# Written order on ACT and VectorE in one group of an up projection and in the last two products, and one ring of tiles for two kinds of data

## The chip, the cores and the metric

One core of a Trainium2 chip runs the whole program. The metric is the device time of one execution in microseconds (us); the profile below is of one such execution, and its times count from the start of its span.

## The reference

One decoder layer on 1024 tokens of width 1024, in float32: a token mixer, then an MLP with squared ReLU (up to 4096, back to 1024), then a last RMSNorm. The change touches the MLP and the last norm:

```python
x = x + jnp.concatenate([y_pool, y_hgrn], axis=-1) @ w_out[l]
h2 = rms_norm(x, norm_mlp_g[l])
x = x + jnp.square(jax.nn.relu(h2 @ w_up[l])) @ w_down[l]
return rms_norm(x, final_norm_g)
```

## The kernel before, in words

**Arithmetic.** Each float32 operand is split into a high part, a cast on ACT (`split`, L116), and a low part, a subtraction on VectorE (L117). A product is then three matmuls: high by high, high by low, low by high (`mm3`, L122 to L124), so the third one (L124) needs the low part of the weights. Both matrix products of the MLP are done in groups of seven products by Strassen's scheme. Sums and differences of quarters are formed first, and the seven results are added into four quarters.

**Up projection.** The hidden width is cut into 8 groups. A group has seven products, each with 24 matmuls of 128x512 in two PSUM banks. Group 0 takes them in the order 1, 2, 5, 6, 3, 7, 4; the others in 1, 5, 6, 3, 7, 2, 4. Product n needs an operand made of quarters of h2.T (`operand(n)`, tiles `h2op_n`) and one made of w_up (`up_weights(n)`: a sum `wsum` or `wdif`, then the split into `whi`, `wlo`). The h2 operands are made once, around group 0, from four tiles `quad`, each 128 x 4 x 512, that `mlp_input` fills with transposes from PE and `mixed_blocks` turns into the sums. For 5 that happens row block by row block; for 6, 3, 7 and 4 as whole tiles of 2048 columns.

**Results of a product.** `sums_out` takes them out of PSUM: ACT copies a bank (products 1, 5, 6; L869 where the profile names it), VectorE adds a bank to what is there (2, 7, 3), product 4 goes through ReLU. Products 1, 6, 7 and 4 use the banks `ps_ua`, 5 and 3 the banks `ps_uc`, 2 the banks `ps_ub`. A later product adds onto what its banks hold, so it may start only when the result of the earlier one has been taken out: product 6 waits for the copies of 1, 3 for those of 5, 7 for those of 6, and 4 for the adds of 7. Finished quarters (`h11`, `h22`, `h12`, `h21`, and the sums `hs3`, `hs2`, `hs4`) go to DRAM over POOL's queue. In the kernel before they have a pool of their own, `hq`, of eight tiles of 128 x 2 x 512, and the pool `quadp` ends when group 0's operands are made.

**Down projection.** Four groups of seven products with 48 matmuls each, in four banks, in the order 1, 5, 3, 6, 7, 2, 4. Their results are added into x, row block by row block. In the last group the row blocks become final one after another. Then come the square sum of the row (ACT, L925), its mean (VectorE, L699 and L701), the power -1/2 (POOL, L704), the scaling of the left half (VectorE, L940) and of the right half (ACT, L938), and two stores.

**Order of the work.** PE's order is written by hand throughout (`manual_schedule`). ACT's, VectorE's and POOL's order in the two projections is chosen by the scheduler that builds the program. Every engine runs its instructions in that fixed order. An instruction that waits for a semaphore holds up what stands behind it on its engine.

Of the kernel before, what the change touches and what calls it, by code (L numbers as in the profile page):

```python
# [10 lines left out]
F32 = mybir.dt.float32  # L11
# [6 lines left out]
P = 128  # L18
# [42 lines left out]
def kernel(  # L61
# [605 lines left out]

    rawp = tc.alloc_tile_pool(name="rawp", bufs=2, reuse_waits="tile")
    sums = tc.alloc_tile_pool(name="sums", bufs=2, reuse_waits="tile")
    with ExitStack() as pb:  # L670
        quadp = pb.enter_context(tc.tile_pool(name="quadp", bufs=4, reuse_waits="tile"))
        g2 = bcast_row(norm_mlp_g, "g2")


# [63 lines left out]
        def mixed_blocks(i):  # L738


            b11, b12, b21, b22 = (quad[k][:, :, i % 4 * P:(i % 4 + 1) * P] for k in ((0, 0), (0, 1), (1, 0), (1, 1)))
            sub(b11, b12, b11)
            split(*(t[:, :, i % 4 * P:(i % 4 + 1) * P] for t in h2[5]), b11)
            sub(b11, b22, b11)
            sub(b12, b22, b12)
            sub(b21, b21, b11)

        def product_out(step, dh):
# [89 lines left out]
        operand(3, big, quad[1, 1])  # L838
        operand(7, big2, quad[0, 1])
        operand(4, big2, quad[1, 0])  # L840

    with ExitStack() as pc:
        hq = pc.enter_context(tc.tile_pool(name="hq", bufs=8, reuse_waits="tile"))

        def up_group(g, order):
            if g:
# [4 lines left out]
            c = {}  # L851
            store, at = hid_out[g // 2], slice(g % 2 * 2, g % 2 * 2 + 2)

            def quarter(name):
                return hq.tile([P, 2, 512], F32, tag="hq", name=f"{name}_{g}")

            def relu2(t):
                dve.scalar_tensor_tensor(out=t, in0=t, scalar=0.0, in1=t, op0=ALU.max, op1=ALU.mult)
# [56 lines left out]
    with ExitStack() as pd:  # L915
# [5 lines left out]
        xs, sss = [None] * NT, [[] for _ in range(NT)]  # L921

        def squares(i, cs, name):
            ss = small.tile([P, 1], F32, tag="ss3", name=f"ss3_{i}_{name}", bufs=16)
            act.activation(junk[:, :cs.stop - cs.start], xs[i][:, cs], AF.Square, accum_out=ss)  # L925
            sss[i].append(ss)

        def final_scale(i, dh, y):
            cs = slice(dh * 512, (dh + 1) * 512)
            dve.tensor_tensor(out=y[:, cs], in0=xs[i][:, cs], in1=gf[:, cs], op=ALU.mult)  # L930

        def final_rows(i, y):

            r = rstd_of_parts(sss[i], f"n3_{i}")
            for h in range(2):
                cs = slice(h * 512, (h + 1) * 512)
                if h:
                    act.mul(y[:, cs], y[:, cs], r)  # L938
                else:
                    dve.scalar_tensor_tensor(out=y[:, cs], in0=xs[i][:, cs], scalar=r, in1=gf[:, cs], op0=ALU.mult, op1=ALU.mult)  # L940
                (nc.sync, act)[h].dma_start(out[0, i * P:(i + 1) * P, cs], y[:, cs])
# [40 lines left out]
        groups, banks, ys, scales, finals = {}, {}, {}, [], []
        products = [(g, n) for g in range(DOWN_GROUPS) for n in DOWN_ORDER]
        ahead = operands(*products[0])
        for at, (g, n) in enumerate(products):
            last = g == DOWN_GROUPS - 1
            pools, a, b = ahead
            if at + 1 < len(products):
                ahead = operands(*products[at + 1])
            if last and n == DOWN_ORDER[-2]:  # L990
                for i in scales:
                    final_scale(i, 1, ys[i])
# [4 lines left out]
            for e in range(4):  # L997
                ps, tc_ = banks[g, key][e], slice(e * P, (e + 1) * P)
                for k in range(4):
                    mm3(ps, (a[0][:, k, tc_], a[1][:, k, tc_]), (b[0][:, k, :], b[1][:, k, :]), fresh and k == 0, k == 3, not fresh)  # L1000

                for i, dh in {1: [(e, 0)], 5: [(e + 4, 1)], 3: [(e, 1)], 6: [(e, 1)], 7: [(e + 4, 1)], 2: [(e, 0)], 4: [(e + 4, 0)]}[n]:
                    cs = slice(dh * 512, (dh + 1) * 512)
                    add(xs[i][:, cs], ps, xs[i][:, cs])
                    if last and n in (6, 7, 2, 4):
                        squares(i, cs, dh)

                        ys[i] = groups[g][0][i // 4][:, i % 4, :]
                        if n in (6, 7):
                            scales.append(i)  # L1010
                        else:
                            finals.append(i)
                            if len(finals) > 1:
                                final_rows(finals[-2], ys[finals[-2]])
# [58 lines left out]
```

## Time and profile before

| | |
|---|---|
| median of 3 runs | 1109.58 us (1108.75 to 1110.09) |
| the profiled execution's own time | 1108.45 us |
| its span | 1106.7 us |
| PE busy | 1082.3 us, 98% of the span |
| VectorE busy | 790.9 us, 71% |
| ACT busy | 422.6 us, 38% |
| up projection, group 0 | about 476.7 to 525 us |
| rest of up, and down | 525 to 1095.6 us |
| after the last matmul | 1095.6 to 1106.7 us |

The time of a run is the span and what lies around it, here 1.75 us. PE's busy time counts matmuls that overlap one another, so 98% says only that PE seldom stands still. In the rows, L with a number is a line of the kernel before; PE is the matmul engine, DVE is VectorE, ACT is ScalarE, POOL is GpSimd.

### The profile page before, as it was taken

The page shows a single profiled execution, that of the slowest core. Times are in us where ns is not written, and L with a number is a line of the kernel's source. Part 1 is how long each engine was busy: PE and PEld are TensorE (multiplying, and loading weights), DVE is VectorE, ACT ScalarE, POOL GpSimd, SP SyncE. Part 2 cuts the span into 40 slices and gives each one's busy share as a digit, 9 for nine tenths or more (in the row PEclk, how much of TensorE's full clock was granted, in tenths as well). Part 3 has the DMA queues.
Part 4 walks back from the last instruction along what each step waited for, and adds up shares of the span by engine and source line. Part 5 has one row for each costly group of instructions (what it writes and reads, how often), then busy time and mean ns, then how long its engine had stood idle before and what let it go on. Part 6 is the DMA issues. An engine that isn't in the chain of part 4 may idle for free.

```text
span 1106.7 us, 14288 instructions
## 1 busy us (share of the span) xinstructions
PE 1082.3 (98%) x5728; PEld 895.0 (81%) x5728; DVE 790.9 (71%) x1068; ACT 422.6 (38%) x647; POOL 81.9 (7%) x124
## 2 busy tenths in 40 slices
PE   8999999999999999999999999999999999999996
PEld 6868797879787788877888888888888888888884
DVE  4498837784779852698568557855988968677774
ACT  6844333434332522353332233224244333324243
POOL 1001010101010111100011001001100000000001
PEclk9999999999999999999999999999999999999998
DMA  9521011110110162324354344427984354353104
GB/s 310 157 58 38 21 39 38 40 38 20 58 39 20 58 219 96 105 77 132 115 190 171 107 159 176 148 95 264 366 344 166 114 190 152 114 197 145 38 1 152
DMA packets 71362, 137.55 MB, mean 124 GB/s; under 512 B 4864, under 2 KB 44928, under 8 KB 67712
## 3 DMA queue, kind: packets, MB, share of 16 engines
q1 hardware_dynamic: 60656, 100.98, 26.8%
q0 software_dynamic: 9344, 33.56, 7.8%
q10 hardware_dynamic: 1296, 2.10, 0.5%
q8 instruction: 45, 0.74, 0.3%
q14 instruction: 21, 0.17, 0.1%
HBM read 98.87 MB, written 37.75 MB: 123 GB/s over the span
## 4 chain that ended last, share of the span: by engine, by line
PE 78%; DVE 12%; issue 3%; ACT 2%; DMA 2%; POOL 1%; SPq 0%; POOLq 0%; DVEq 0%; ACTq 0%
PE ps_dx L122 5%; PE ps_dx L124 5%; PE ps_dx L123 5%; PE ps_ua L122 5%; PE ps_ua L123 5%; PE ps_ua L124 5%; PE ps_dy L122 3%; PE ps_dy L124 3%; PE ps_dy L123 3%; PE ps_uc L123 2%; PE ps_uc L122 2%; PE ps_uc L124 2%; PE ps_o L122 2%; PE ps_o L123 2%; PE ps_o L124 2%
## 5 line engine op out<-in xcount | busy, mean ns | idle before, releaser
L116 ACT CAST wdop<-raw_wd 128x2048 fp32r<-128x2048 f32 x28 | 53.5, 1912 | 154.4 <-PE ps_dy L124 47.2
L122 PE MATMUL ps_ua<-h2op,whi_wu 128*128 128x512 f32 x256 | 100.1, 391 | 3.2 <-ACT h L869 2.7
L123 PE MATMUL ps_ua<-h2op,whi_wu 128*128 128x512 f32 x256 | 99.7, 389 | 0.0
L124 PE MATMUL ps_ua<-h2op,wlo_wu 128*128 128x512 f32 x256 | 99.7, 389 | 0.0
L123 PE MATMUL ps_dx<-wdop,hop 128*128 128x512 f32 x256 | 99.6, 389 | 0.0
L124 PE MATMUL ps_dx<-wdop,hop 128*128 128x512 f32 x256 | 99.6, 389 | 0.0
L122 PE MATMUL ps_dx<-wdop,hop 128*128 128x512 f32 x256 | 99.6, 389 | 0.0
L117 DVE TENSOR_TENSOR wdop<-raw_wd,wdop 128x2048 fp32r<-128x2048 f32 x28 | 64.1, 2290 | 28.6 <-ACT wdop L116 28.6
L117 DVE TENSOR_TENSOR wlo_wu<-raw_wu,whi_wu 128x1024 fp32r<-128x1024 f32 x24 | 29.2, 1222 | 55.0 <-ACT whi_wu L116 55.0
L117 DVE TENSOR_TENSOR hop<-hraw,hop 128x2048 fp32r<-128x2048 f32 x28 | 63.9, 2283 | 4.5 <-ACT hop L116 4.5
L116 ACT CAST hop<-hraw 128x2048 fp32r<-128x2048 f32 x28 | 53.4, 1909 | 30.7 <-DMA hraw<-hid 22.4
L116 ACT CAST whi_wu<-wsum 128x1024 fp32r<-128x1024 f32 x24 | 25.3, 1054 | 99.3 <-DVE wsum L659 49.0
L122 PEld LDWEIGHTS ps_ua<-h2op,whi_wu 128*128 128x128 f32 x256 | 48.1, 188 | 14.2 <-ACT h L869 3.1
L124 PEld LDWEIGHTS ps_dx<-wdop,hop 128*128 128x128 f32 x256 | 48.1, 188 | 10.0
L124 PEld LDWEIGHTS ps_ua<-h2op,wlo_wu 128*128 128x128 f32 x256 | 48.1, 188 | 10.0
L123 PEld LDWEIGHTS ps_dx<-wdop,hop 128*128 128x128 f32 x256 | 48.1, 188 | 10.0
L122 PE MATMUL ps_v<-whi_v,hT_hi 128*128 128x256 f32 x192 | 54.5, 285 | 1.6 <-ACT whi_v L116 1.5
L122 PEld LDWEIGHTS ps_dx<-wdop,hop 128*128 128x128 f32 x256 | 48.1, 188 | 9.9
L123 PEld LDWEIGHTS ps_ua<-h2op,whi_wu 128*128 128x128 f32 x256 | 48.1, 188 | 9.8
L662 DVE TENSOR_TENSOR x<-ps_dx,x 128x512 f32<-128x512 f32 x64 | 43.9, 686 | 16.4 <-PE ps_dx L124 16.4
L123 PE MATMUL ps_v<-wlo_v,hT_hi 128*128 128x256 f32 x192 | 54.3, 284 | 0.8 <-DVE wlo_v L117 0.8
L124 PE MATMUL ps_v<-whi_v,hT_lo 128*128 128x256 f32 x192 | 54.1, 284 | 0.0
(230 smaller groups left out, 2779.2 us busy)
## 6 DMA issues: line engine op xcount, KB each, us to landing
hraw<-hid SPq DMA_DIRECT2D x28, 1024.0 KB, 5.3
raw_wu<-in_w_up_dram SPq DMA_DIRECT2D x32, 512.0 KB, 3.7
hid<-h POOLq DMA_DIRECT2D x32, 512.0 KB, 3.2
raw_wd<-in_w_down_dram SPq DMA_DIRECT2D x16, 1024.0 KB, 7.2
hid<-hs POOLq DMA_DIRECT2D x24, 512.0 KB, 3.4
xt<-in_x_t_dram SPq DMA_DIRECT2D x8, 512.0 KB, 7.8
xn<-in_x_dram SPq DMA_DIRECT2D x8, 512.0 KB, 6.8
x<-x_mid SPq DMA_DIRECT2D x8, 512.0 KB, 6.5
```

Of the source, the lines that this page charges most:

```text
L116: act.copy(hi, src)
L117: dve.tensor_tensor(out=lo, in0=src, in1=hi.bitcast(F32), op=ALU.subtract)
L122: pe.matmul(ps, lh, rh, start=start, stop=False, skip_group_check=goes_on)
L123: pe.matmul(ps, lh, rl, start=False, stop=False, skip_group_check=goes_on)
L124: pe.matmul(ps, ll, rh, start=False, stop=stop, skip_group_check=goes_on)
L662: dve.tensor_tensor(out=out_, in0=a, in1=b, op=ALU.add)
```

## The change

There are three parts. First, the hidden quarters no longer have a pool: `quadp` lives through the whole up projection, and a quarter is one half of a tile of that ring of four. Pairs share a tile: h11 and h22; h12 and hs3; h21 and hs4; hs2 has one alone. Second, in group 0 ACT and VectorE run in the order in which the code is written. `up_weights(6)` now stands ahead of the last `mlp_input`, operand 6 ahead of the first results, and operands and weights of 3, 7 and 4 are each written one product ahead of their use. Third, the last two down products have written order on VectorE, ACT and POOL; a row's mean starts from a right half that was worked out earlier, and the rows 4 to 7 are put out from a tile `y` of their own.

```diff
+    quadp = tc.alloc_tile_pool(name="quadp", bufs=4, reuse_waits="tile")
...
-        quadp = pb.enter_context(tc.tile_pool(name="quadp", bufs=4, reuse_waits="tile"))
...
             sub(b11, b12, b11)
+            sub(b12, b22, b12)
             split(*(t[:, :, i % 4 * P:(i % 4 + 1) * P] for t in h2[5]), b11)
             sub(b11, b22, b11)
-            sub(b12, b22, b12)
             sub(b21, b21, b11)
...
+        steady = tc.manual_schedule(engines={mybir.EngineType.DVE, mybir.EngineType.Activation})
+        steady.__enter__()
         for n, key in ((1, "a"), (2, "b")):
...
             if n == 1:
+                split_first[6] = up_weights(0, 6, w_first, s_first)
                 mlp_input(7)
                 mixed_blocks(7)
-        operand(6, big, quad[0, 0])
-        split_first[6] = up_weights(0, 6, w_first, s_first)
-        operand(3, big, quad[1, 1])
-        operand(7, big2, quad[0, 1])
-        operand(4, big2, quad[1, 0])
-
-    with ExitStack() as pc:
-        hq = pc.enter_context(tc.tile_pool(name="hq", bufs=8, reuse_waits="tile"))
+
+        later = {6: (big, quad[0, 0]), 3: (big, quad[1, 1]), 7: (big2, quad[0, 1]), 4: (big2, quad[1, 0])}
...
             def quarter(name):
-                return hq.tile([P, 2, 512], F32, tag="hq", name=f"{name}_{g}")
+
+                place = {"h11": 0, "h22": 0, "h12": 1, "hs3": 1, "hs2": 2, "h21": 3, "hs4": 3}[name]
+                if place not in pairs:
+                    pairs[place] = [quadp.tile([P, 2, 2, 512], F32, tag="quad", name=f"hid_{g}_{place}"), 0]
+                t, n = pairs[place]
+                pairs[place][1] += 1
+                return t[:, n]
...
-            for n in order:
+            for at_, n in enumerate(order):
                 key = {1: "a", 6: "a", 7: "a", 4: "a", 5: "c", 3: "c", 2: "b"}[n]
+                if g == 0:
+                    for m in order[3:at_ + 3] or order[3:4]:
+                        if m in later:
+                            operand(m, *later.pop(m))
+                            if m not in ready:
+                                ready[m] = up_weights(g, m, w, s)
                 if g == 0 and n in (1, 2):
...
             up_group(g, ORDER if g else FIRST_ORDER)
+            if g == 0:
+                steady.__exit__(None, None, None)
+    quadp.release()
...
+        def right_half(i, y):
+
+            ss = small.tile([P, 1], F32, tag="part", name=f"ss_{i}", bufs=8)
+            dve.tensor_scalar(ss, squares(i, 1), 1.0 / D, EPS, op0=ALU.mult, op1=ALU.add)
+            sss[i] = ss
+            ys[i] = y
+            dve.tensor_tensor(out=y[:, 512:], in0=xs[i][:, 512:], in1=gf[:, 512:], op=ALU.mult)
+
+        def row_scale(i, ss):
+            ms = small.tile([P, 1], F32, tag="ms", name=f"ms_n3_{i}")
+            dve.tensor_scalar(ms, ss, 1.0 / D, sss[i], op0=ALU.mult, op1=ALU.add)
...
+                rows = [groups[g][0][0], places.pop(0).tile([P, 4, D], F32, tag="big", name="y")]
...
+        with tc.manual_schedule(engines={mybir.EngineType.DVE, mybir.EngineType.Activation, mybir.EngineType.Pool}):
+            pools, a, b = ahead
+            ahead = operands(*products[-1])
+            ready = None
+            for (g, n), (pools, a, b) in zip(products[-2:], ((pools, a, b), ahead)):
+                for i in product(g, n, a, b):
+                    ss = squares(i, 0)
+                    if ready:
+                        final_rows(*ready)
+                    ready = i, row_scale(i, ss)
+            final_rows(*ready)
```

The order that results on ACT, in group 0, from where VectorE forms the last h2 sums (whi_wu_0_n: high part of the weights of product n in group 0; h2op_n: operand n; h11_0, h22_0, h12_0: hidden quarters). Before:

```order
L116 CAST h2op_5_4179<-quad_00_3702 128x4x128
L116 CAST h2op_7_4476<-quad_01_3700 128x2048
L116 CAST h2op_6_4465<-quad_00_3702 128x2048
L116 CAST h2op_3_4473<-quad_11_3703 128x2048
L116 CAST h2op_4_4479<-quad_10_3701 128x2048
L869 COPY h11_0_4486<-ps_ua_0_0_4395 128x512
L869 COPY h11_0_4486<-ps_ua_0_1_4396 128x512
L869 COPY h22_0_4507<-ps_uc_0_0_4493 128x512
L869 COPY h22_0_4507<-ps_uc_0_1_4494 128x512
L116 CAST whi_wu_0_3_4550<-wsum_0_4389 128x1024
L116 CAST whi_wu_0_7_4583<-wdif_0_4581 128x1024
L116 CAST whi_wu_0_4_4623<-raw_wu_0_11_4379 128x1024
```

And of the change, where hid_0_0 is the tile of h11 and h22, and hid_0_1 that of h12:

```order
L116 CAST h2op_6_4472<-quad_00_3702 128x2048
L872 COPY hid_0_0_4475<-ps_ua_0_0_4397 128x512
L872 COPY hid_0_0_4475<-ps_ua_0_1_4398 128x512
L116 CAST h2op_3_4482<-quad_11_3703 128x2048
L116 CAST whi_wu_0_3_4486<-wsum_0_4389 128x1024
L872 COPY hid_0_0_4475<-ps_uc_0_0_4490 128x512
L872 COPY hid_0_0_4475<-ps_uc_0_1_4491 128x512
L116 CAST h2op_7_4518<-quad_01_3700 128x2048
L116 CAST whi_wu_0_7_4523<-wdif_0_4521 128x1024
L872 COPY hid_0_1_4539<-ps_ua_0_0_4397 128x512
L872 COPY hid_0_1_4539<-ps_ua_0_1_4398 128x512
L116 CAST h2op_4_4554<-quad_10_3701 128x2048
```

The four casts of h2 stood in a row, ahead of the copies out of PSUM and of the weights of 3, 7 and 4; now those of 3, 7 and 4 stand each just ahead of the weights of the same product, and copies lie between.

VectorE in group 0, up to its first add of product 7 (the one that frees the bank in which product 4 starts; wlo is the low part of weights, wsum_1, wdif_1 and wlo_wu_1_n belong to group 1). Before:

```order
L858 SCALAR_TENSOR_TENSOR h11_0_4486<-h11_0_4486 128x1024
L117 TENSOR_TENSOR wlo_wu_0_3_4551<-wsum_0_4389,whi_wu_0_3_4550 128x1024
L117 TENSOR_TENSOR wlo_wu_0_7_4584<-wdif_0_4581,whi_wu_0_7_4583 128x1024
L117 TENSOR_TENSOR wlo_wu_0_4_4624<-raw_wu_0_11_4379,whi_wu_0_4_4623 128x1024
L117 TENSOR_TENSOR wlo_wu_1_1_4671<-raw_wu_1_00_4660,whi_wu_1_1_4670 128x1024
L662 TENSOR_TENSOR wsum_1_4703<-raw_wu_1_10_4664,raw_wu_1_11_4666 128x1024
L662 TENSOR_TENSOR h12_0_4534<-ps_uc_0_0_4493,h12_0_4534 128x512
L659 TENSOR_TENSOR wdif_1_4800<-raw_wu_1_00_4660,raw_wu_1_10_4664 128x1024
L662 TENSOR_TENSOR h12_0_4534<-ps_uc_0_1_4494,h12_0_4534 128x512
L858 SCALAR_TENSOR_TENSOR h12_0_4534<-h12_0_4534 128x1024
L117 TENSOR_TENSOR wlo_wu_1_5_4706<-wsum_1_4703,whi_wu_1_5_4705 128x1024
L662 TENSOR_TENSOR h22_0_4507<-ps_ua_0_0_4395,h22_0_4507 128x512
```

And of the change:

```order
L659 TENSOR_TENSOR wsum_0_4389<-raw_wu_0_01_4375,wsum_0_4389 128x1024
L117 TENSOR_TENSOR wlo_wu_0_3_4487<-wsum_0_4389,whi_wu_0_3_4486 128x1024
L117 TENSOR_TENSOR h2op_7_4518<-quad_01_3700,h2op_7_4518 128x2048
L659 TENSOR_TENSOR wdif_0_4521<-raw_wu_0_00_4373,raw_wu_0_10_4377 128x1024
L117 TENSOR_TENSOR wlo_wu_0_7_4524<-wdif_0_4521,whi_wu_0_7_4523 128x1024
L117 TENSOR_TENSOR h2op_4_4554<-quad_10_3701,h2op_4_4554 128x2048
L117 TENSOR_TENSOR wlo_wu_0_4_4558<-raw_wu_0_11_4379,whi_wu_0_4_4557 128x1024
L662 TENSOR_TENSOR hid_0_1_4539<-ps_uc_0_0_4490,hid_0_1_4539 128x512
L662 TENSOR_TENSOR hid_0_1_4539<-ps_uc_0_1_4491,hid_0_1_4539 128x512
L117 TENSOR_TENSOR wlo_wu_1_1_4667<-raw_wu_1_00_4656,whi_wu_1_1_4666 128x1024
L861 SCALAR_TENSOR_TENSOR hid_0_1_4539<-hid_0_1_4539 128x1024
L662 TENSOR_TENSOR hid_0_0_4475<-ps_ua_0_0_4397,hid_0_0_4475 128x512
```

The low parts of 3, 7 and 4 stood side by side, and three instructions for group 1 (wsum_1, wdif_1, wlo_wu_1_5) lay ahead of the last row; now the h2 subtractions of 7 and 4 lie between the low parts, and the three instructions for group 1 come later.

VectorE at the end of the program (x_i: row block i; rstd_n3_i: its scale; ps_dx: the banks of the last product). Before:

```order
L699 TENSOR_SCALAR ms0_n3_7_8337<-ss3_7_1_8124 128x1
L940 SCALAR_TENSOR_TENSOR raw_wd_3_1_7736<-x_6_6461,rstd_n3_6_8331,gf_6441 128x512
L662 TENSOR_TENSOR x_7_6463<-ps_dx_3_3_7811,x_7_6463 128x512
L701 SCALAR_TENSOR_TENSOR ms1_n3_7_8339<-ss3_7_0_8325,ms0_n3_7_8337 128x1
L940 SCALAR_TENSOR_TENSOR raw_wd_3_1_7736<-x_7_6463,rstd_n3_7_8341,gf_6441 128x512
```

And of the change:

```order
L950 TENSOR_SCALAR ms_n3_6_8294<-ss3_6_0_8288,ss_6_8103 128x1
L662 TENSOR_TENSOR x_7_6438<-ps_dx_3_3_7786,x_7_6438 128x512
L957 SCALAR_TENSOR_TENSOR y_7973<-x_6_6436,rstd_n3_6_8296,gf_6416 128x512
L950 TENSOR_SCALAR ms_n3_7_8317<-ss3_7_0_8311,ss_7_8121 128x1
L957 SCALAR_TENSOR_TENSOR y_7973<-x_7_6438,rstd_n3_7_8319,gf_6416 128x512
```

The add of row block 7 stood behind the scaling of row block 6, and stands ahead of it now.

## Rows read from the trace of the kernel before

**Rows 1.** The page's first part: busy time of each engine over the span, its share, and the number of instructions.

```profile
PE 1082.3 (98%) x5728; PEld 895.0 (81%) x5728; DVE 790.9 (71%) x1068; ACT 422.6 (38%) x647; POOL 81.9 (7%) x124
```

**Rows 2.** [...]

```profile
476.70:506.70 30.00, 25.55 (x119) 20.59 (x118) 29.21 (x31) 19.90 (x24) 1.73 (x3) 1.00 0.26 89
506.70:510.10 3.40, 3.40 (x9) 2.66 (x9) 2.38 (x3) 0.27 (x1) 0.00 (x0) 0.51 0.45 120
...
525.00:1095.60 570.60, 570.60 (x2518) 472.31 (x2516) 418.78 (x390) 196.66 (x194) 31.44 (x59) 1.00 0.45 163
1095.60:1106.70 11.10, 0.02 (x1) 0.00 (x0) 2.49 (x6) 2.72 (x6) 1.08 (x2) 0.73 0.38 142
```

**Rows 3.** What PE waited for between 476 and 525 us: total, times, longest.

```profile
PE ps_ua L122 <- ACT h L869: 2.7, 1, 2.7
PE ps_uc L124 <- DVE wlo_wu L117: 1.8, 1, 1.8
PE ps_ua L122 <- DVE h L662: 0.5, 1, 0.5
```

**Rows 4.** PE's instructions in group 0, in order of time: start, duration, what it is, and in brackets the idle time before it and its releaser.

```profile
494.63 0.39 PE L124 MATMUL ps_uc<-h2op,wlo_wu 128*128 128x512 f32 x1
497.69 0.50 PE L122 MATMUL ps_ua<-h2op,whi_wu 128*128 128x512 f32 x1 [2.68 <-ACT h L869]
...
505.73 0.50 PE L124 MATMUL ps_uc<-h2op,wlo_wu 128*128 128x512 f32 x1 [1.78 <-DVE wlo_wu L117]
...
507.20 0.63 PE L123 MATMUL ps_uc<-h2op,whi_wu 128*128 128x512 f32 x1
507.63 0.63 PE L124 MATMUL ps_uc<-h2op,wlo_wu 128*128 128x512 f32 x1
...
512.46 0.39 PE L122 MATMUL ps_ua<-h2op,whi_wu 128*128 128x512 f32 x1
...
517.67 0.39 PE L124 MATMUL ps_ua<-h2op,wlo_wu 128*128 128x512 f32 x1
518.55 0.50 PE L122 MATMUL ps_ua<-h2op,whi_wu 128*128 128x512 f32 x1 [0.49 <-DVE h L662]
```

**Rows 5.** VectorE in group 0, in the same form; x4 or x2 marks neighbours that are merged into one row.

```profile
492.06 8.89 DVE L117 TENSOR_TENSOR h2op<-quad,h2op 128x2048 fp32r<-128x2048 f32 x4
500.87 1.22 DVE L659 TENSOR_TENSOR wsum<-raw_wu,wsum 128x1024 f32<-128x1024 f32 x1
...
503.32 1.23 DVE L858 SCALAR_TENSOR_TENSOR h<-h 128x1024 f32<-128x1024 f32 x1
...
506.73 2.35 DVE L117 TENSOR_TENSOR wlo_wu<-raw_wu,whi_wu 128x1024 fp32r<-128x1024 f32 x2
511.94 1.23 DVE L662 TENSOR_TENSOR wsum<-raw_wu,raw_wu 128x1024 f32<-128x1024 f32 x1 [2.86 <-DMA raw_wu<-in_w_up_dram]
...
513.68 1.22 DVE L659 TENSOR_TENSOR wdif<-raw_wu,raw_wu 128x1024 f32<-128x1024 f32 x1
...
516.68 1.22 DVE L117 TENSOR_TENSOR wlo_wu<-wsum,whi_wu 128x1024 fp32r<-128x1024 f32 x1
517.81 0.68 DVE L662 TENSOR_TENSOR h<-ps_ua,h 128x512 f32<-128x512 f32 x1
```

**Rows 6.** ACT in group 0, in the same form.

```profile
486.89 1.05 ACT L116 CAST whi_wu<-wsum 128x1024 fp32r<-128x1024 f32 x1 [2.10 <-DVE wsum L659]
...
489.83 7.33 ACT L116 CAST h2op<-quad 128x2048 fp32r<-128x2048 f32 x4 [1.37 <-DVE quad L659]
497.06 1.06 ACT L869 COPY h<-ps_ua 128x512 f32<-128x512 f32 x2
...
502.12 1.05 ACT L116 CAST whi_wu<-wsum 128x1024 fp32r<-128x1024 f32 x1 [2.20 <-DVE wsum L659]
```

**Rows 7.** DMA issues: KB of each, and median us from issue to landing.

```profile
raw_wu<-in_w_up_dram SPq DMA_DIRECT2D x32, 512.0 KB, 3.7
hid<-h POOLq DMA_DIRECT2D x32, 512.0 KB, 3.2
```

**Rows 8.** All engines at the end of the program, in order of time; ACTq is the queue of DMAs that ACT issues.

```profile
1094.72 0.68 DVE L662 TENSOR_TENSOR x<-ps_dx,x 128x512 f32<-128x512 f32 x1
...
1095.23 0.39 PE L124 MATMUL ps_dx<-wdop,hop 128*128 128x512 f32 x1
...
1097.00 0.72 ACT L938 ACTIVATE raw_wd<-raw_wd,rstd_n 128x512 f32<-128x512 f32 x1 [0.84 <-POOL rstd_n L704]
1097.00 0.75 DVE L940 SCALAR_TENSOR_TENSOR raw_wd<-x,rstd_n,gf 128x512 f32<-128x512 f32 x1 [0.59 <-POOL rstd_n L704]
1097.67 0.68 DVE L662 TENSOR_TENSOR x<-ps_dx,x 128x512 f32<-128x512 f32 x1
...
1098.39 0.63 ACT L925 ACTIVATE junk<-x 128x512 bf16<-128x512 f32 x1 [0.67 <-DVE x L662]
...
1099.14 0.16 DVE L701 SCALAR_TENSOR_TENSOR ms_n<-ss,ms_n 128x1 f32<-128x1 f32 x1 [0.79 <-ACT junk L925]
1099.38 0.54 POOL L704 TENSOR_TENSOR rstd_n<-ms_n,nhalf 128x1 f32<-128x1 f32 x1 [2.41 <-DVE ms_n L701]
1099.95 0.72 ACT L938 ACTIVATE raw_wd<-raw_wd,rstd_n 128x512 f32<-128x512 f32 x1 [0.85 <-POOL rstd_n L704]
...
1100.71 0.37 ACTq L941 DMA_DIRECT2D out_dram<-raw_wd  x1
```

More of the change, by code (lines that the diff above doesn't have):

```diff
@@ L850, in up_group @@
                 w, banks, s, ready = w_first, dict(first), s_first, split_first
-            c = {}
+            c, pairs = {}, {}
             store, at = hid_out[g // 2], slice(g % 2 * 2, g % 2 * 2 + 2)
             def quarter(name):
-                return hq.tile([P, 2, 512], F32, tag="hq", name=f"{name}_{g}")
+                place = {"h11": 0, "h22": 0, "h12": 1, "hs3": 1, "hs2": 2, "h21": 3, "hs4": 3}[name]
[4 more added lines that the diff above has]
+                return t[:, n]
             def relu2(t):
@@ L920 @@
         places = [big, big, big, big2, big2, big, big2]
[L921 to L941, printed above, removed]
+        xs, sss = [None] * NT, [None] * NT
@@ new lines, in squares @@
+        def squares(i, dh):
+            ss = small.tile([P, 1], F32, tag="ss3", name=f"ss3_{i}_{dh}", bufs=16)
+            act.activation(junk, xs[i][:, dh * 512:(dh + 1) * 512], AF.Square, accum_out=ss)
+            return ss
+        def right_half(i, y):
[4 more added lines that the diff above has]
+            dve.tensor_tensor(out=y[:, 512:], in0=xs[i][:, 512:], in1=gf[:, 512:], op=ALU.mult)
@@ new lines, in row_scale, with final_rows @@
+        def row_scale(i, ss):
+            ms = small.tile([P, 1], F32, tag="ms", name=f"ms_n3_{i}")
+            dve.tensor_scalar(ms, ss, 1.0 / D, sss[i], op0=ALU.mult, op1=ALU.add)
+            r = small.tile([P, 1], F32, tag="rstd", name=f"rstd_n3_{i}")
+            pool.tensor_tensor(out=r, in0=ms, in1=nhalf[:, :1], op=ALU.pow)
+            return r
+        def final_rows(i, r):
+            y = ys[i]
+            dve.scalar_tensor_tensor(out=y[:, :512], in0=xs[i][:, :512], scalar=r, in1=gf[:, :512], op0=ALU.mult, op1=ALU.mult)
+            act.mul(y[:, 512:], y[:, 512:], r)
+            nc.sync.dma_start(out[0, i * P:(i + 1) * P, :512], y[:, :512])
+            act.dma_start(out[0, i * P:(i + 1) * P, 512:], y[:, 512:])
@@ L980, in operands, with product @@
             return pools, a, b
[L982 to L992, printed above, removed]
+        def product(g, n, a, b):
             key = "y" if n in (5, 3) else "z" if n == 2 else "x"
@@ L1000 @@
                     mm3(ps, (a[0][:, k, tc_], a[1][:, k, tc_]), (b[0][:, k, :], b[1][:, k, :]), fresh and k == 0, k == 3, not fresh)
[L1002 to L1014, printed above, removed]
+                i, dh = {1: (e, 0), 5: (e + 4, 1), 3: (e, 1), 6: (e, 1), 7: (e + 4, 1), 2: (e, 0), 4: (e + 4, 0)}[n]
+                cs = slice(dh * 512, (dh + 1) * 512)
+                add(xs[i][:, cs], ps, xs[i][:, cs])
+                yield i
+        groups, banks, ys = {}, {}, {}
+        products = [(g, n) for g in range(DOWN_GROUPS) for n in DOWN_ORDER]
+        ahead = operands(*products[0])
+        for at, (g, n) in enumerate(products[:-2]):
+            last = g == DOWN_GROUPS - 1
+            pools, a, b = ahead
+            ahead = operands(*products[at + 1])
+            if last and n == 6:
+                rows = [groups[g][0][0], places.pop(0).tile([P, 4, D], F32, tag="big", name="y")]
+            for i in product(g, n, a, b):
+                if last and n in (6, 7):
+                    right_half(i, rows[i // 4][:, i % 4, :])
             places += pools
@@ L1017 @@
                 places.append(groups[g][1].pop(0))
-        final_rows(finals[-1], ys[finals[-1]])
+        with tc.manual_schedule(engines={mybir.EngineType.DVE, mybir.EngineType.Activation, mybir.EngineType.Pool}):
+            pools, a, b = ahead
+            ahead = operands(*products[-1])
+            ready = None
+            for (g, n), (pools, a, b) in zip(products[-2:], ((pools, a, b), ahead)):
+                for i in product(g, n, a, b):
+                    ss = squares(i, 0)
[3 more added lines that the diff above has]
+            final_rows(*ready)
 _INS = [
```

## The prediction

> **What bounds the kernel now.** I began with the totals. PE is busy for 1082.3 of 1106.7 us, VectorE for 790.9 and ACT for 422.6 [rows 1]. An average hides stages with different limits, so the next view was the busy time by stretch. From 525 to 1095.6 us PE is busy for the whole 570.60 us [rows 2]. No edit there that leaves the matmuls alone can bring the end forward; it can only bring a stop. That leaves two places: group 0 of the up projection, and the end.
>
> In group 0 the waits name three stops of PE: 2.7 us for a copy of h11 by ACT, 1.8 us for the low part of a weight, 0.5 us for an add of VectorE [rows 3]. The timeline shows where: ahead of products 6 (497.69) and 3 (505.73), and ahead of 4 (518.55). In between is a stretch without any wait in which matmuls start 0.43 us apart (507.20, 507.63), where product 7 has 23 steps in 5.21 us, 0.227 each [rows 4]. [...] From the last matmul of product 5 (494.63) to the first of product 4 there are 73 steps, 16.6 us at 0.227; they took 23.9. So 7.4 us is lost: the three waits, about 1.6 us of slow clock (8 steps at 0.2 us extra), and the restarts.
>
> Why PE waits is seen on the other two. VectorE has no gap worth naming from 492 to 509; four h2 subtractions in a row take 8.89 us [rows 5]. ACT casts the same four in 7.33 us, and the copies that product 6 wants stand behind them, at 497.06 [rows 6]. So it is a matter of order on two full engines, and the account to draw up is VectorE's.
>
> At the end, the last matmul starts at 1095.23 and is done 0.39 us later. VectorE, though, scales row block 6 first (1097.00) and adds the last bank at 1097.67. From there the square (1098.39), the mean (1099.14), the power (1099.38), the scaling (1099.95) and the last store (1100.71) follow in a chain [rows 8].
>
> **Group 0 after the change.** Unit prices, all from [rows 5, 6]: VectorE 0.68 us for 512 columns, 1.22 for 1024, 2.22 for 2048 in a row (8.89/4); ACT 0.53 for a copy (1.06/2), 1.05 for a cast of 1024, 1.83 for one of 2048 (7.33/4). A hand-off costs 0.03 to 0.05: VectorE ends the sum of 500.87 at 502.09, ACT starts at 502.12. VectorE's work from 482 us to the add that frees product 4's bank is the same as before, but for three instructions of group 1 that the written order puts behind it (wsum_1, wdif_1, wlo_wu_1_5). They are the rows at 511.94, 513.68 and 516.68: 3 x 1.14 from start to start, 3.4 us. With them goes the 2.86 us that the first of them waited for a load. Without new gaps that add, which ended at 518.49, would end at 518.49 - 2.86 - 3.4 = 512.2.
>
> Now the gaps that the written order makes. Wherever VectorE's next instruction needs a cast that itself needs VectorE's last one, it stands still for the cast and two hand-offs. Going down the new order:
> first, wlo of 6 needs whi of 6, which needs the sum just made: 1.05 + 0.1, less 0.6 for a subtraction that runs meanwhile, 0.55;
> second, h2op_6 needs a cast of 2048 that starts when the last sum is there: 1.9, less 0.6 of other work, 1.3;
> third, the h11 adds need ACT's copy, which begins once h2op_6 is done (the ring gives the tile only then): 0.53 + 0.1, about 0.7;
> fourth and sixth, wlo of 3 and of 7: each needs the cast of a sum made just before, 1.05 + 0.1 = 1.15, twice 2.3;
> fifth and seventh, h2op_7 and h2op_4: ACT does two copies (1.06) and the cast (1.83) after whi, 2.8 with the hand-offs, while VectorE has only a wlo of 1.22 to do, 1.6, twice 3.2.
> These are 8.05 us. The instruction ahead of each gap takes its full duration and not its step to the next start (1.22 against 1.14, 0.68 against 0.60), seven times 0.07, 0.5 us. So the add ends at 512.2 + 8.05 + 0.5 = 520.75, and product 4 starts at about 520.8 in place of 518.55: **+2.3 us**. The bounds: if the hand-offs hide in half of the gaps, 0.7 less; if ACT's queue pushes each pair of copies one further, 0.5 us more twice. I take +2.3, between +1.5 and +3.3.
>
> The products before do better than now and it is worth nothing. Product 6 starts at about 496.3, when h2op_6 and the first copy are there; 3 at about 503.8; 7 at about 511.2, with its L124 at 511.9 and its end at 511.9 + 22 x 0.227, about 517. PE then stands still for almost 4 us ahead of 4. A slow clock in products 3 or 7 would hide in this wait. If the wait were gone, it would cost 1.6 us for each.
>
> What comes late through this: group 1's three instructions and the loads behind them. Two weights of group 1 can be loaded only when wdif of 0 (now about 509) and wlo of 4 (about 516.9) have read their buffers. A load lands in 3.7 us [rows 7], so at 513 and 521, and product 1 of group 1 starts after 526. Nothing waits.
>
> **The clock behind the wait.** Before, PE stopped for 2.7 and 1.8 us and then ran at 0.51 for 3.4 us [rows 2, 3]. The new wait of 4 us is longer than either, and product 4 lies right behind it with nothing to hide a slow stretch: PE is full from there on. I take the same price, 8 steps at 0.2, **+1.6 us**. The bounds are 0 (behind the first stop, of 2.7 us, there was no slow stretch: the granted clock is 1.00 up to 506.7 [rows 2]) and about 3.2 (two such stretches).
>
> [...]
>
> **The end.** The written order puts the last add ahead of the scaling of row block 6. It follows the last matmul: 1095.23 + 0.39 + 0.04, so 1095.66 in place of 1097.67, 2.0 us earlier. The chain behind it stays: square, mean, power, scaling. One new thing stands on ACT: the scaling of block 6 (0.72) and its store come between the square and the last scaling. The square runs 1096.38 to 1097.1, the scaling of 6 to 1097.8, the issue of the store to about 1098.15 (0.37), the last scaling to 1098.87; the last store goes out at 1098.9 against 1100.71. That is 1.8; without the cost of the issue it is 2.0. I take **-1.9 us**. Bounds: 0 (if the last stores are held by the ones ahead of them in the queues) to 2.0. The mean loses one of its two small instructions per row, which lie under PE's work except for the last row; counted in the chain.
>
> **The ring.** The hidden quarters have four tiles of 2048 in place of eight of 1024, the same space. In group 0 this gives the third gap above. Later, h11 of a group must wait until h22 of the group before, in the same tile, has been used and written. A write takes 3.2 us [rows 7]. The copy of h11 is wanted by the third product of a group, two products or 10.9 us after the group begins. I take 0.
>
> **Sum.** +2.3 + 1.6 - 1.9 = +2.0 us. Against the profiled execution's own 1108.45 us that is 1110.45. The median of the runs is 1109.58, 1.1 higher, so the forecast on that scale is **1111.6 us**, 0.18% above before. A change of 0.2%, 2.2 us, is about what a measurement of this kernel can tell from none.
>
> **Rivals.**
> The clock does not fall (or falls where the wait hides it): +2.3 - 1.9 = +0.4, 1110.0. For it speaks the first stop; against it that product 4 has nothing before it but the longest stop. 0.15.
> The stops go, the kernel is faster. This is the other side. If VectorE's gaps are shorter than worked out, product 4 starts earlier: with none of them at 512.2, which is -6.3, with the end -8.2, 1101.4. For it speaks that products 6, 3 and 7 all start earlier than before. It decides if the gaps come to less than 6 us in place of 8.55, so that product 4 starts before 518.2 and the clock stays up. Against it: each gap is an instruction that needs another engine's result, at durations from rows. 0.10.
> [...]
> The clock falls twice, or for longer: +2.3 + 3.2 - 1.9 = +3.6, 1113.2. 0.10.
> The end gains nothing, since the last stores are held by those ahead: +3.9, 1113.5. The spacing of the chain speaks against it. 0.08.
> The ring holds a copy until a write has landed, by more than the slack, in the seven later groups: 1 us in each gives +9, 1118.6. Against it stand 10.9 us of slack for a write of 3.2. 0.05.
> The forecast itself has 0.52, with a range of its own from 1110.4 to 1113.
>
> **How the numbers follow.** The forecast lies just inside the bound of 0.2%: of its 0.52 I count 0.30 as no change and 0.22 as slower. The first rival gives 0.13 no change, 0.02 faster; the second 0.10 faster; the other three, 0.23, are slower. Together: faster 0.12, same 0.43, slower 0.45. The range leaves out the faster rival, most of the ring's, and the ends of the others: 1109.2 to 1113.8.
>
> **What would show it.** In the changed kernel's profile: product 6 of group 0 starts at about 496.3, 3 at 503.8, 7 at 511.2, 4 at 520.8 with a wait of 3 to 4 us for an add of VectorE. VectorE has seven gaps of 0.5 to 1.6 us there, each ended by ACT. A stretch at half clock follows the start of product 4. From then to the last matmul PE has no idle time. The last add starts 0.4 us after the last matmul, the last store goes out 3.7 us after the start of the last matmul. The prediction is wrong if product 4 starts before 518, if PE stops in a later group, or if the store goes out no sooner than now (5.5 us after that start).

## The result, and the profile after

The changed kernel takes 1112.2 us (median of 22 runs, 1111.08 to 1115.75) against 1110.24 us for the kernel before (median of 22 runs taken beside it): the ratio is 1.0019, with a 95% interval from 1.0012 to 1.0025. The medians differ by 1.96 us; the forecast was 2.0 more, 1111.6 on the scale of 1109.58.

PE's matmuls stand in the same order in every kernel here, but for the 15 that one experiment adds. So the same matmul can be looked up in each trace, and the span falls into six parts (all in us; group 0 runs from its first matmul to the first of group 1):

| profiled execution | first 400 matmuls | from there to group 0 | group 0, start to product 4 | product 4 | later matmuls | end | span |
|---|---|---|---|---|---|---|---|
| before | 70.96 | 406.55 | 41.04 | 5.71 | 570.97 | 11.44 | 1106.7 |
| changed | 71.86 | 406.64 | 43.53 | 7.17 | 570.97 | 9.50 | 1109.7 |
| difference | +0.90 | +0.09 | +2.49 | +1.46 | 0.00 | -1.94 | +3.0 |

The first two columns are not the change: both kernels have the same instructions there. In the traces of this study the first 400 matmuls took 70.96 to 72.77 us, whatever the kernel; two traces of one kernel (the end alone, below) have 72.77 and 71.11. Without those 0.99 us the difference of the two profiles is +2.0 us.

What PE waited for in group 0 of the changed kernel (total, times, longest):

```profile
PE ps_ua L122 <- DVE hid L662: 3.8, 1, 3.8
PE ps_uc L122 <- ACT hid L872: 1.8, 1, 1.8
PE ps_uc L122 <- ACT h2op L116: 0.4, 1, 0.4
```

The stop of 2.7 us ahead of product 6 [rows 3] is gone and product 3 still has one of 1.8 us, now ahead of its first matmul and for ACT's copy; the 0.4 us are ahead of product 5; ahead of product 4 there are 3.8 us where there were 0.5. Where the products start, and what follows the last stop (start, duration, instruction, idle time before it):

```profile
497.32 0.50 PE L122 MATMUL ps_ua<-h2op,whi_wu 128*128 128x512 f32 x1
...
504.80 0.50 PE L122 MATMUL ps_uc<-h2op,whi_wu 128*128 128x512 f32 x1 [1.75 <-ACT hid L872]
...
512.35 0.39 PE L122 MATMUL ps_ua<-h2op,whi_wu 128*128 128x512 f32 x1
...
522.03 0.47 PE L122 MATMUL ps_ua<-h2op,whi_wu 128*128 128x512 f32 x1 [3.83 <-DVE hid L662]
...
523.77 0.63 PE L122 MATMUL ps_ua<-h2op,whi_wu 128*128 128x512 f32 x1
524.20 0.63 PE L123 MATMUL ps_ua<-h2op,whi_wu 128*128 128x512 f32 x1
```

Times of this trace are 0.99 us late against [rows 4]. Less that, products 6, 3, 7 and 4 start at 496.33, 503.81, 511.36 and 521.04. Ahead of product 4 PE stands still, and behind its start the matmuls are 0.43 apart (523.77, 524.20). The busy time by stretch (start and end, length; busy time and instructions of PE, of its weight loads, of VectorE, ACT and POOL; the clock granted to PE as a share of full speed; the DMA share and GB/s; [rows 2] have the same columns):

```profile
506.20:509.50 3.30, 3.30 (x9) 2.62 (x8) 2.43 (x2) 0.84 (x1) 0.00 (x0) 0.50 0.01 5
509.50:523.30 13.80, 9.96 (x42) 7.57 (x42) 11.13 (x11) 5.72 (x6) 0.00 (x0) 0.99 0.38 114
523.30:526.60 3.30, 3.30 (x9) 2.58 (x8) 3.30 (x4) 1.04 (x1) 0.96 (x2) 0.50 0.14 57
526.60:1100.50 573.90, 573.90 (x2532) 475.05 (x2531) 424.97 (x397) 198.75 (x197) 32.08 (x61) 1.00 0.45 165
```

Two stretches run at 0.50: one in product 3 (506.2 to 509.5 us), and one in product 4 (523.3 to 526.6). From 526.6 us to the last matmul PE is busy for the whole time, as in [rows 2].

VectorE in group 0 of the changed kernel:

```profile
488.42 1.23 DVE L117 TENSOR_TENSOR wlo_wu<-wsum,whi_wu 128x1024 fp32r<-128x1024 f32 x1 [0.57 <-ACT whi_wu L116]
...
494.35 2.29 DVE L117 TENSOR_TENSOR h2op<-quad,h2op 128x2048 fp32r<-128x2048 f32 x1 [1.25 <-ACT h2op L116]
497.30 1.29 DVE L662 TENSOR_TENSOR hid<-ps_ub,hid 128x512 f32<-128x512 f32 x2 [0.65 <-ACT hid L872]
...
504.30 1.23 DVE L117 TENSOR_TENSOR wlo_wu<-wsum,whi_wu 128x1024 fp32r<-128x1024 f32 x1 [1.11 <-ACT whi_wu L116]
507.07 2.29 DVE L117 TENSOR_TENSOR h2op<-quad,h2op 128x2048 fp32r<-128x2048 f32 x1 [1.55 <-ACT h2op L116]
...
511.62 1.23 DVE L117 TENSOR_TENSOR wlo_wu<-wdif,whi_wu 128x1024 fp32r<-128x1024 f32 x1 [1.12 <-ACT whi_wu L116]
514.39 2.29 DVE L117 TENSOR_TENSOR h2op<-quad,h2op 128x2048 fp32r<-128x2048 f32 x1 [1.55 <-ACT h2op L116]
...
521.20 1.28 DVE L662 TENSOR_TENSOR hid<-ps_ua,hid 128x512 f32<-128x512 f32 x2
```

Where [rows 5] had one gap, there are seven, each ended by ACT: 0.57, 1.25, 0.65, 1.11, 1.55, 1.12 and 1.55 us, 7.8 in all. The third is the ring's, since the copy on ACT that ends it starts only when VectorE has done the h2 subtraction of 494.35, at 496.64:

```profile
496.68 1.07 ACT L872 COPY hid<-ps_ua 128x512 f32<-128x512 f32 x2 [2.36 <-DVE h2op L117]
```

The end of the changed kernel, all engines:

```profile
1100.17 0.39 PE L124 MATMUL ps_dx<-wdop,hop 128*128 128x512 f32 x1
1100.60 0.69 DVE L662 TENSOR_TENSOR x<-ps_dx,x 128x512 f32<-128x512 f32 x1 [1.02 <-PE ps_dx L124]
...
1101.32 0.63 ACT L937 ACTIVATE junk<-x 128x512 bf16<-128x512 f32 x1 [1.38 <-DVE x L662]
...
1102.08 0.21 DVE L950 TENSOR_SCALAR ms_n<-ss,ss 128x1 f32<-128x1 f32 x1
1102.37 0.54 POOL L952 TENSOR_TENSOR rstd_n<-ms_n,nhalf 128x1 f32<-128x1 f32 x1 [2.18 <-DVE ms_n L950]
...
1102.68 0.34 ACTq L960 DMA_DIRECT2D out_dram<-y  x1
1102.95 0.75 DVE L957 SCALAR_TENSOR_TENSOR y<-x,rstd_n,gf 128x512 f32<-128x512 f32 x1 [0.66 <-POOL rstd_n L952]
1103.07 0.72 ACT L958 ACTIVATE y<-y,rstd_n 128x512 f32<-128x512 f32 x1 [0.42 <-POOL rstd_n L952]
1103.82 0.34 ACTq L960 DMA_DIRECT2D out_dram<-y  x1
```

The last add now follows the last matmul at once (1100.60 against 1100.17 for the matmul's start; before 1097.67 against 1095.23 [rows 8]). The last store goes out 3.65 us after the start of the last matmul, where it took 5.48.

### The profile page after: what moved, and what is told of

It reads as the page before. It is cut to its first block, busy times and chain, and to the rows that moved or that the text cites. A ratio compares the mean times of both kernels' runs of the same rounds, so it can differ in the third digit from the quotient of the medians.

```text
span 1109.7 us, 14274 instructions
## 1 busy us (share of the span) xinstructions
PE 1084.5 (98%) x5728; PEld 896.0 (81%) x5728; DVE 792.5 (71%) x1068; ACT 422.2 (38%) x647; POOL 81.9 (7%) x124
## 4 chain that ended last, share of the span: by engine, by line
PE 80%; DVE 11%; issue 3%; ACT 3%; DMA 2%; POOL 1%; SPq 0%; ACTq 0%; POOLq 0%; DVEq 0%
PE ps_dx L123 5%; PE ps_dx L124 5%; PE ps_dx L122 5%; PE ps_ua L122 5%; PE ps_ua L124 5%; PE ps_ua L123 5%; PE ps_dy L123 3%; PE ps_dy L124 3%; PE ps_dy L122 3%; PE ps_uc L124 2%; PE ps_uc L122 2%; PE ps_uc L123 2%; PE ps_o L122 2%; PE ps_o L124 2%; PE ps_o L123 2%
```

## The experiments

Two theories were tested. The first is that of the prediction: VectorE's gaps set the start of product 4, a slow clock follows PE's stop, and the end gives back 1.9 us. The other holds that the parts act on each other or that the time has another place: the ring, written order as such, or the stores.

**The ring and group 0, with the old end.** The last two down products are built as before.

```diff
-        with tc.manual_schedule(engines={mybir.EngineType.DVE, mybir.EngineType.Activation, mybir.EngineType.Pool}):
...
+        for at, (g, n) in enumerate(products):
...
```

> This is the changed kernel with the last two down products as before (scheduler's order, row sums as before), so only the ring and the written order of group 0 remain. My account (VectorE's gaps 2.3 us, slow clock behind the wait 1.6 us, end -1.9 us): without the end it is +3.9 us against the kernel before, ratio 1.0035; product 4 of group 0 starts 2.3 us later than before against product 1's start. The rival that the end gains nothing: +2.0 us, ratio 1.0018, like the full change.

Measured: 1113.79 us (11 runs) against 1110.94, ratio 1.0030 (1.0019 to 1.0041). By the parts of its trace, group 0 up to product 4 takes 43.51, product 4 7.15 and the end 11.44: +3.9 us against before, all of it in group 0. The rival's 1.0018 lies just outside the interval, and the trace decides against it.

**The end alone.** The kernel before with only the new end; run twice.

```diff
-            if last and n == DOWN_ORDER[-2]:
-                for i in scales:
-                    final_scale(i, 1, ys[i])
+            if last and n == 6:
+                rows = [groups[g][0][0], places.pop(0).tile([P, 4, D], F32, tag="big", name="y")]
...
+        with tc.manual_schedule(engines={mybir.EngineType.DVE, mybir.EngineType.Activation, mybir.EngineType.Pool}):
```

> The kernel before with only the end changed (the last two products in written order, the row means from the earlier right half). My account: -1.9 us, ratio 0.9983; the last add 0.4 us after the last matmul and the last store 3.7 us after the last matmul's start, group 0 as before. The rival that the last stores are held by those ahead: 0, ratio 1.000.

Measured: 1107.57 us (5 runs), ratio 0.9964 (0.9952 to 0.9977), more than forecast. Its trace has an end of 9.49 us, 1.95 less than before. In group 0 ACT and VectorE have the order of before, product 4 starts after 40.97 us and takes 5.72, as before. So it was run again.

> The same kernel as tail_only, which measured 0.9964 (0.9952 to 0.9977) where its trace shows only 1.95 us less at the end than before, 0.9982. If the trace tells all, the ratio is near 0.9982 this time; if the new end is worth more in the executions that were not profiled, again near 0.9964.

Measured: 1108.21 us (11 runs), ratio 0.9982 (0.9973 to 0.9992), as the trace says. The second run has twice as many executions; the first figure is not explained by anything seen in the traces. The same kernel has thus given two ratios that lie 0.0018 apart, so a ratio from four to six executions, as two of those below are, can be off by more than its interval says; the parts of the traces carry more there.

**The ring alone.** Quarters in the ring, order by the scheduler, old end.

```diff
-                return hq.tile([P, 2, 512], F32, tag="hq", name=f"{name}_{g}")
+                place = {"h11": 0, "h22": 0, "h12": 1, "hs3": 1, "hs2": 2, "h21": 3, "hs4": 3}[name]
+                if place not in pairs:
+                    pairs[place] = [quadp.tile([P, 2, 2, 512], F32, tag="quad", name=f"hid_{g}_{place}"), 0]
```

> The kernel before with only the ring: hidden quarters in the four quad tiles, no written order in group 0, old end. My account takes the ring's waits at 0: ratio 1.000 (within 0.0007). In the order that the scheduler now builds, ACT has the copies of product 6 ahead of the weights of product 3, so that product 3 may start up to 1 us later than before: at most +1 us. The rival that the ring holds copies in the later groups until writes have landed: 1 us in each of seven groups, +7 us, ratio 1.006, with PE idle after 525 us.

Measured: 1110.92 us (11 runs), ratio 0.9995 (0.9985 to 1.0006). Product 4 starts 40.98 us after group 0, and the later matmuls take 570.97 us, as before: PE has no wait for writes. The rival of the ring falls.

**Ring and end, without the written order in group 0.**

```diff
-        steady = tc.manual_schedule(engines={mybir.EngineType.DVE, mybir.EngineType.Activation})
-        steady.__enter__()
```

> The changed kernel without the written order in group 0: ring and new end only. By my account 0 and -1.95 us, ratio 0.9982. Against the changed kernel (1.0019) it shows what the written order of group 0 costs by itself: 4 us. The rival that the parts act on each other: anything outside 0.997 to 0.9995.

Measured: 1108.44 us (11 runs), ratio 0.9979 (0.9971 to 0.9988). Against the change's 1.0019 the written order of group 0 costs 0.0040, 4.4 us, give or take 1.2 us by the two intervals. Between the two profiled executions group 0 differs by 3.0 us (50.70 and 47.67), since this one had two slow stretches in it (last section).

**The casts one place earlier.** Order as in the change; only the casts of three operands on ACT are moved.

```diff
-                            operand(m, *later.pop(m))
+                            operand_hi(m)
+                            operand_lo(m)
+                            if m in after_:
+                                operand_hi(after_[m])
```

> The changed kernel, but in group 0 ACT's casts of the h2 operands 3, 7 and 4 stand one place earlier: each behind the split of the operand ahead of it instead of just ahead of its own subtraction. All else as in the change. If VectorE's gaps set the start of product 4, the two gaps of 1.55 us ahead of h2op_7 and h2op_4 go and the others stay: product 4 starts 3.1 us earlier than in the changed kernel, and PE's wait ahead of it falls from 3.8 to about 0.7 us. If the slow clock stays away with so short a wait, that is -4.6 us against the changed kernel and -2.6 against before (ratio 0.9977); if it comes nevertheless, -3.1 and -1.1 (0.9990). The rival that something else than VectorE's order holds product 4: as the changed kernel, 1.0019.

Measured: 1106.72 us (6 runs), ratio 0.9965 (0.9953 to 0.9978). VectorE's two subtractions now follow without a gap (505.50 + 2.28, 511.18 + 2.29), and the gaps ahead of the weights are as they were:

```profile
504.36 1.22 DVE L117 TENSOR_TENSOR wlo_wu<-wsum,whi_wu 128x1024 fp32r<-128x1024 f32 x1 [1.11 <-ACT whi_wu L116]
505.50 2.28 DVE L850 TENSOR_TENSOR h2op<-quad,h2op 128x2048 fp32r<-128x2048 f32 x1
...
510.04 1.23 DVE L117 TENSOR_TENSOR wlo_wu<-wdif,whi_wu 128x1024 fp32r<-128x1024 f32 x1 [1.12 <-ACT whi_wu L116]
511.18 2.29 DVE L850 TENSOR_TENSOR h2op<-quad,h2op 128x2048 fp32r<-128x2048 f32 x1
```

PE's waits in the same kernel:

```profile
PE ps_ua L122 <- DVE hid L662: 2.2, 1, 2.2
PE ps_uc L122 <- ACT hid L882: 1.7, 1, 1.7
PE ps_uc L122 <- ACT h2op L116: 0.4, 1, 0.4
```

Product 4 starts 40.25 us after group 0, 3.28 earlier than in the change, where 3.1 was forecast. The wait ahead of it is 2.2 us and not the 0.7 of the expectation: in this execution no stretch of group 0 runs at the low clock, so product 7 ends earlier too:

```profile
476.00:517.50 41.50, 38.10 (x169) 29.57 (x167) 35.83 (x39) 20.29 (x24) 1.74 (x3) 1.00 0.25 82
517.50:530.00 12.50, 11.19 (x49) 9.31 (x50) 12.50 (x14) 3.91 (x6) 2.67 (x5) 1.00 0.43 170
```

Product 4 takes 5.54 us instead of 7.17. By the parts this is -0.96 us in group 0 and -1.94 at the end against before, ratio 0.9974, inside the interval.

**Matmuls in PE's wait.** 15 more matmuls, into a bank that is no longer read.

```diff
+                    if g == 0 and n == 4:
+                        for _ in range(15):
+                            pe.matmul(banks["b"][0], ready[7][0][:, 0, :P], h2[7][0][:, 0, :], start=True, stop=True)
```

> The changed kernel with 15 matmuls more on PE between products 7 and 4 of group 0, 15 x 0.227 = 3.4 us of PE's wait of 3.8. They write a bank that nobody reads any more. The order of ACT and VectorE is that of the change, so product 4 starts when it does there. If the slow stretch behind product 4's start comes from PE's standing still ahead of it, it is gone: -1.5 us against the changed kernel, +0.5 against before (ratio 1.0005). If the low clock has another cause, or the price lies in the wait alone: as the changed kernel, 1.0019, or a little above.

Measured: 1110.06 us (11 runs), ratio 0.9993 (0.9984 to 1.0002). PE around product 4, and the busy time by stretch:

```profile
517.22 0.39 PE L124 MATMUL ps_ua<-h2op,wlo_wu 128*128 128x512 f32 x1
517.44 3.56 PE L899 MATMUL ps_ub<-h2op,whi_wu 128*128 128x512 f32 x15
521.45 0.47 PE L122 MATMUL ps_ua<-h2op,whi_wu 128*128 128x512 f32 x1 [0.45 <-DVE hid L662]
```

```profile
505.80:509.20 3.40, 3.40 (x9) 2.64 (x8) 2.71 (x2) 0.66 (x1) 0.00 (x0) 0.51 0.01 4
...
517.10:530.00 12.90, 12.46 (x56) 9.99 (x55) 12.90 (x15) 3.39 (x5) 1.60 (x3) 1.00 0.42 155
```

Product 4 starts 43.53 us after group 0, as in the change. Behind it the granted clock is 1.00, and the product takes 5.56 us, 1.61 less. So here the slow stretch in product 4 came with PE's standing still, and its price in the traces is 1.6 us. The timed gain is larger than forecast: from 1.0019 to 0.9993 are 2.9 us, and the expected 1.0005, like the +0.4 us of the trace's parts (1.0004), lies just above the interval. What the other 1.3 us are the runs do not show.

**Another written order.** The casts of operands 3 and 7 stand on ACT before they are wanted; the sums of 3 and 7 are formed side by side; the adds of products 2 and 3 come behind the operands of 4. The order in which it is written:

```diff
+                mlp_input(7)
+                sub(b11, b12, b11)
+                sub(b12, b22, b12)
+                act.copy(hi5, b11)
+                sub(s_first[0], s_first[0], w_first[0, 0])
+                low(lo5, hi5, b11)
+                sub(b11, b22, b11)
+                sub(b21, b21, b11)
+                operand_hi(3)
+                weights_hi(6, s_first[0])
+                operand_hi(6)
+                operand_lo(3)
+                operand_lo(6)
+                weights_lo(6, s_first[0])
+                operand_hi(7)
...
+                if g == 0 and n == 5:
+                    sub(s[0], w[0, 1], s[0])
+                    weights_hi(3, s[0])
+                    s[1] = sums.tile([P, 4, 256], F32, tag="sum", name=f"wdif_{g}")
+                    sub(s[1], w[0, 0], w[1, 0])
+                    weights_lo(3, s[0])
+                    weights_hi(7, s[1])
+                    operand_lo(7)
+                    weights_lo(7, s[1])
+                if g == 0 and n == 6:
+                    operand_hi(4)
+                    weights_hi(4, w[1, 1])
+                    operand_lo(4)
+                    weights_lo(4, w[1, 1])
```

> The changed kernel (ring, written order, new end) with another written order in group 0: the casts of operands 3 and 7 stand on ACT before they are wanted, the sums of 3 and 7 are formed side by side, and the adds of products 2 and 3 stand behind the operands of 4. Nothing is left out. If VectorE's gaps are what costs (my account), product 4 starts at about 511 us on the clock of the kernel before, PE has next to no wait in group 0 and no slow clock there: -7.4 and -1.9, -9.3 us, ratio 0.9916. If a written order as such or the ring costs the time, it is no faster than the changed kernel, ratio 1.0019.

Measured: 1100.99 us (4 runs), ratio 0.9912 (0.9893 to 0.9930). PE's waits in group 0 are down to one of 0.5 us:

```profile
PE ps_ua L124 <- DVE wlo_wu L832: 0.5, 1, 0.5
```

VectorE, in the same kernel, over the stretch that had the gaps:

```profile
490.86 4.48 DVE L832 TENSOR_TENSOR h2op<-quad,h2op 128x2048 fp32r<-128x2048 f32 x2
495.27 1.22 DVE L832 TENSOR_TENSOR wlo_wu<-wsum,whi_wu 128x1024 fp32r<-128x1024 f32 x1
496.52 1.22 DVE L659 TENSOR_TENSOR wsum<-raw_wu,wsum 128x1024 f32<-128x1024 f32 x1
...
498.86 1.22 DVE L832 TENSOR_TENSOR wlo_wu<-wsum,whi_wu 128x1024 fp32r<-128x1024 f32 x1
500.00 2.28 DVE L832 TENSOR_TENSOR h2op<-quad,h2op 128x2048 fp32r<-128x2048 f32 x1
...
503.34 2.28 DVE L832 TENSOR_TENSOR h2op<-quad,h2op 128x2048 fp32r<-128x2048 f32 x1
...
510.65 1.23 DVE L662 TENSOR_TENSOR wsum<-raw_wu,raw_wu 128x1024 f32<-128x1024 f32 x1 [0.42 <-DMA raw_wu<-in_w_up_dram]
```

The gaps are gone: from 490.86 no start lies more than 0.03 us behind the end of the row ahead, until a load is waited for at 510.65. Product 4 starts 34.52 us after group 0: 144 matmuls at 0.2265 are 32.6, the eight transposes between products 1 and 2 take 0.8, the one stop 0.5, and the slower steps behind these the rest, 0.6. PE, and no longer VectorE, sets this start. Group 0 takes 40.23 us against 46.75 before, 6.5 less where 7.4 were expected, and the end 9.50 against 11.44: -8.5 us by the trace. By the timed ratio it is 9.8 us less, with an interval of 7.8 to 11.9. This kernel beats both, and the ring and the written order are in it. It moves other instructions besides closing the gaps (the adds of products 2 and 3), so it does not price the gaps alone; the casts one place earlier do that for two of them.

## Why the prediction was right

**Product 4 by VectorE's account.** Forecast +2.3, measured +2.49. The gaps held one by one: forecast as 0.55, 1.3, 0.7, 1.15, 1.6, 1.15, 1.6 (8.05), they are 0.57, 1.25, 0.65, 1.11, 1.55, 1.12, 1.55 (7.80). With what the account adds for full durations they were to delay the add by 8.55 us from 512.2. It ends at 520.9 on the same scale, 8.7 later: the gaps are 0.25 less, and three short waits of 0.03 to 0.10 us around 490 to 492, which the account does not have, cost about 0.3 with the overlap that they undo. The starts of products 6, 3, 7 and 4, forecast at 496.3, 503.8, 511.2 and 520.8, are 496.33, 503.81, 511.36 and 521.04 on the same scale. Without two of the gaps (casts ahead) product 4 came 3.28 us earlier, 3.1 forecast. In the other order, which has none of them, it came 9.0 us earlier, by more than the gaps, since other instructions moved too. That a gap delays what stands behind it is seen in the kernel before: the first add of product 3 (513.08) stands behind the sum that waited 2.86 us for its load [rows 5], and it starts only behind that sum, though the last matmul of its bank had started at 508.91 and VectorE stood still up to 511.94:

```profile
508.91 0.63 PE L124 MATMUL ps_uc<-h2op,wlo_wu 128*128 128x512 f32 x1
...
513.08 0.68 DVE L662 TENSOR_TENSOR h<-ps_uc,h 128x512 f32<-128x512 f32 x1
```

**The clock behind the wait.** Forecast +1.6, measured +1.46 in the profile and 1.61 by the matmuls that filled the wait. The bound of 0 did not come true: both profiles with the stop of 3.8 us have the slow stretch (product 4 takes 7.17 and 7.15 us), and the first rival's +0.4 us (1.0004) lies outside the measured interval. With the wait filled the granted clock stays at 1.00 from 517.1 to 530 us. Why the clock falls no run shows.

**The slow clock in product 3.** The prediction let it hide in the wait ahead of 4, and so it did: behind a stretch at 0.50 from 506.2 product 7 starts 0.16 us later than forecast, without a wait ahead of it, and still ends 3.8 us before VectorE lets product 4 start. That its start agrees so well is luck: from 503.8 on, 24 matmuls at 0.227 end near 509.2, so the forecast of 511.2 has PE wait there, and in the trace the slow clock fills that time.

**The end.** Forecast -1.9 (-1.8 by the queue, -2.0 without the issue), measured -1.94 in the changed kernel, -1.95 alone. The issue of the store ahead of it (1102.68 to 1103.02) costs the last scaling little: ACT starts it at 1103.07, 0.12 us after VectorE starts its own half (1102.95). The rival that the stores are held falls.

**The ring.** Forecast 0 in the later groups; alone it measured 0.9995 (0.9985 to 1.0006). Its one cost that was forecast, the third gap under the written order, came to 0.65 us of the 0.7; no run takes away that gap alone.

**The rival on the other side** named its condition rightly: if the gaps come to less than 6 us, the kernel is faster. With the casts ahead they come to 4.7, and product 4 starts 0.8 us earlier than before; with none the kernel is 0.9% faster, where the rival had -8.2 us with the end and the trace has -8.5.

**What was a little off.** The terms miss by +0.19, -0.14 and -0.04 us, so that their sum fits to 0.01 is in part luck; the interval of the timed ratio is 1.3 to 2.8 us. PE's short stops in product 5 (0.4 and 0.25 us) are not in the prediction; they come before the later waits and hide in them. The profiled execution of before, 1108.45 us, is the fastest of the 22 (1108.45 to 1112.26); that of the change is 0.7 under its median. The forecast was a difference, so this did no harm; taken from the profiled time straight to a median it would have been 1.8 us too low.

## What to carry to other kernels

Where two engines hand work to each other and a third waits for both, draw up an account of the fuller one: its work up to the instruction that is waited for, less what is moved behind that, plus a cast and two hand-offs for every place where its next instruction needs an answer to its last one. Here that account gave the start of a product to 0.3 us, and it says what to do with a written order: start on the other engine what does not depend on the last result, before it is wanted. A stop of the matmul engine cost its length here and, where nothing hid it, in some profiles a stretch at a granted clock of 0.50 on top: 1.5 to 1.6 us in product 4 behind the stop of 3.8 us, nothing there behind stops of 2.2 us (casts ahead) and 2.0 us (end alone).

## What the runs showed of the hardware that was not expected

The same instructions in the same order did not always get the same clock here. In the kernel of ring and end the profiled execution has two slow stretches in group 0, at 0.50 from 498.3 and from 508.6 us. The ring alone has the same instructions in the same order there on PE, ACT and VectorE, and the same three stops, but one slow stretch. PE's stops, and the slow stretches of ring and end:

```profile
PE ps_ua L122 <- ACT hid L872: 2.7, 1, 2.7
PE ps_uc L122 <- ACT whi_wu L116: 1.6, 1, 1.6
PE ps_uc L124 <- DVE wlo_wu L117: 0.5, 1, 0.5
```

```profile
498.30:501.60 3.30, 2.88 (x7) 2.33 (x8) 3.30 (x2) 1.82 (x4) 0.00 (x0) 0.50 0.02 5
...
508.60:511.90 3.30, 3.21 (x8) 2.53 (x9) 3.30 (x4) 1.62 (x2) 0.00 (x0) 0.50 0.00 1
```

The first lies in product 6, right behind the stop of 2.7 us, where the ring alone has none. With the two, product 4 starts 42.23 us after group 0, where the kernels in the scheduler's order with one such stretch (before, ring alone, end alone twice) have 40.95 to 41.04. The end alone and before share their order in group 0 too: the stretch lies in product 6 in both traces of the first and in product 3 in that of the second, and the time lost by it is hidden ahead of product 4, where the end alone waits 2.0 us for VectorE and before 0.5 [rows 3]:

```profile
PE ps_ua L122 <- DVE h L662: 2.0, 1, 2.0
```

So the row on which the prediction put its bound of 0, no slow stretch behind the first stop, was that of one execution. And behind stops of 2.2, 1.7 and 0.4 us (casts ahead) the profiled execution has none, with a granted clock of 1.00 from 476 to 530 us, where before has one behind stops of 2.7 and 1.8 us, at 0.51 from 506.7 us [rows 2]. What decides this the runs do not show. It may be part of why 22 executions of the kernel before spread over 3.8 us; that was not tested.
